# The sample's MLP in another order: product 4 ahead of 6, a down step inside the last pair, a split last block

## The chip, the cores and the metric

The kernel runs on one core of a Trainium2 chip. The metric is the device time of one execution in microseconds (us). A core has five engines that run side by side, each with a queue of its own that it works off strictly in order: TensorE (PE, matrix products into the accumulator memory PSUM, with its weight loads as PEld), VectorE (DVE), ScalarE (ACT), GpSimd (POOL) and SyncE (SP, which here issues the transfers between the core's memory SBUF and DRAM). They wait for each other through semaphores.

## The reference

One encoder layer for two batches, a prompt of 512 tokens and a sample of 1024, with shared weights, all in float32. The model width is 1024, the MLP's inner width D_FF 2816.

```python
h = _rmsnorm(x, norm_attn_g[l])
z = h @ w_in[l]                       # queries, keys, values, two convolution inputs
a_out = _window_attn(q, k, v, bias, band, attn_sink[l])
c = ca * jax.nn.sigmoid(cb)
c = _dwconv(c, conv_dw_w[l], conv_dw_b[l])
c = jax.nn.silu(_layernorm(c, conv_ln_g[l], conv_ln_b[l]))
x = x + jnp.concatenate([a_out, c], axis=-1) @ w_out[l]
h = _rmsnorm(x, norm_ffn_g[l])
u = _dwconv(h @ w_up[l], ffn_dw_w[l], ffn_dw_b[l])        # 3 taps over tokens
x = x + (jax.nn.silu(u[..., :D_FF]) * u[..., D_FF:]) @ w_down[l]
return _rmsnorm(x, norm_final_g)
```

The change lies in the last four lines, for the sample.

## The kernel before

Products are made in float32 accuracy from parts: each operand is split into a rounded part (hi, a cast on ACT) and the rest (lo, a subtraction on DVE or POOL), and a product is hi·hi + hi·lo + lo·hi, three matmuls of 128 x 128 weights by 512 columns. Until 907 us of the profile the kernel works on the input projection, the attention, the convolution, the prompt's MLP and the sample's out-projection. What follows is the sample's MLP.

*Operands.* `scaled` (line numbers below are those of the code shown at the end of this section) scales the normalised token blocks and forms sums and differences of them, since the MLP's big products are made in a scheme of seven half-size products instead of eight: the tokens, the model width, and the pair gate/value (or, in the down stage, the inner width and the output) are each halved, and sums of halves are multiplied. The seven left operands are transposed by PE, four 128 x 128 blocks at a time (`turned`, L961), cast by ACT (L963) and split by DVE (L918); seven right operands come from the weights by `sums_up` (three sums on DVE, one on POOL) and `split_up` (cast on ACT, L1024, rest on POOL, L918).

*Up stage.* The inner width has 22 column blocks of 128 (j, `NJ`). Each has products 1 to 7 of 12 matmuls (`prod`, L1038 to L1040: four slices of the width by three parts). Products 1 and 2 add up in the left half and 4 in the right half of a PSUM tile x; 5 and 3 in the left, 6 and 7 in the right half of a tile wy. There are four such tiles of two banks, named w0 to w3: blocks of even and odd j take turns, so that x of block j+2 needs the place of x of block j, and wy of j+2 that of wy of j. Between products DVE forms sums with L915: u2 (6 with a copy of 1, made by ACT at L1096), u3 (7 with the same copy), and then the halves of gate and value. `gate_part(j)` makes the three taps of the depthwise convolution of x (L1134 on ACT, L1135 and L1136 on DVE) and a tanh (L1143); the second tap of DVE is what frees x. `value_part(j)` does the same for wy (which it frees), multiplies both into t, and after an odd block forms sums of the pair's t and writes ten blocks to a buffer ga in DRAM.

*Down stage.* For seven products i in the order 1, 2, 5, 6, 7, 4, 3 and 11 pairs p of inner blocks (77 steps) `operands` takes the pair's block from ga and a block of w_down, forms differences, and splits both (`split_of`: cast L922, rest L918 on POOL or DVE); a step is 12 matmuls (L1309 to L1311) into two of the wide tiles. `load_next` issues the loads ahead, `make` the splits, four steps ahead. At the end of a product `evacuate` adds into accumulators, and `with_x` the residual.

*Finish.* `finish(blk, ...)` normalises a block of 128 tokens: a square with a sum of each half on ACT (L1359), three small POOL operations (L1360 to L1362), scaling with the final gain (L1366 and L1367 on ACT and POOL for the left half, L1369 on DVE; in the last two blocks both halves by L1369), stores. The last product is worked off by token blocks: first blocks 0 and 1 together with p, then block 2, then block 3.

*What sets the order.* The program is written in the order of the calls, but the Tile framework's scheduler then puts every engine's queue into an order of its own, from its model of durations, and that order is fixed in the program. So the queues as built, not the order of the calls, tell who stands behind whom.

## Time and profile before

| what | us |
|---|---|
| median of 3 runs (lowest to highest) | 1613.76 (1613.69 to 1615.75) |
| the profiled execution | 1611.46 |
| its span on the core | 1609.4 |
| PE busy in it | 1530.8 |
| sample's MLP: product 1 of block 0 starts | at 908.81 |
| product 7 of block 21, in the last pair, starts | at 1360.74 |
| PE's last matmul ends | at 1594.06 |
| mean granted TensorE clock | 0.989 |

Every time in the rows is from the start of the span. A row of the timeline has the start, the duration (both in us), engine, line, operation, out<-in by the program's names, shape and count; in brackets the idle time before it and what ended it. Matmuls overlap in the rows: each lasts about 0.39 us there, but they start about 0.23 us apart. A row of a group has busy us and mean ns behind the bar, then the idle time before such instructions and its releasers. Buffer letters give the size: h is 512 columns in SBUF, q and c 1024, w the wide PSUM tiles.

### The profile page before, as it was taken

How to read it: one execution, taken by the hardware profiler on the slowest of the kernel's cores; microseconds unless marked ns; L12 is line 12 of the kernel's file. 1: busy time of each engine (PE TensorE's matmuls, PEld its weight loads, DVE VectorE, ACT ScalarE, POOL GpSimd, SP SyncE). 2: the span in 40 equal slices, each digit the busy share in tenths (PEclk: the TensorE clock that was granted, in tenths of full speed). 3: DMA queues.
4: the chain of work that ended last, by engine and by line, in shares of the span. 5: the costliest groups of instructions: out<-in, count | busy, mean ns of one | idle time of the engine just before them, and what ended most of it. 6: DMA issues, size and time to landing. Idle time of an engine off the chain costs nothing. (4 is left out here: it accounts for less than half of the span.)

```text
span 1609.4 us, 20236 instructions
## 1 busy us (share of the span) xinstructions
PE 1530.8 (95%) x6907; PEld 1239.3 (77%) x6907; DVE 1194.1 (74%) x1681; ACT 762.5 (47%) x1356; POOL 881.2 (55%) x673
## 2 busy tenths in 40 slices
PE   8899899999999999999899989999999998999996
PEld 6778788877877878888678767777777777887774
DVE  7989857739898987656666768777776767697685
ACT  4634656244566565555443444343333334444353
POOL 6642354147667766556631435665555555455586
PEclk9999999999999999999999999999999999999998
DMA  7572246365233323334572212333333326875512
GB/s 234 151 206 83 79 122 175 96 186 142 86 99 111 106 81 116 105 99 150 171 255 79 79 53 85 98 99 98 98 99 98 99 72 202 307 252 160 173 51 104
DMA packets 209771, 207.62 MB, mean 129 GB/s; under 512 B 11156, under 2 KB 150748, under 8 KB 209541
## 3 DMA queue, kind: packets, MB, share of 16 engines
q1 hardware_dynamic: 209669, 206.35, 40.7%
q8 instruction: 54, 0.88, 0.2%
q14 instruction: 48, 0.39, 0.1%
HBM read 158.84 MB, written 48.51 MB: 129 GB/s over the span
## 5 line engine op out<-in xcount | busy, mean ns | idle before, releaser
L143 POOL TENSOR_TENSOR q<-q,q 128x1024 fp32r<-128x1024 f32 x72 | 174.9, 2435 | 68.2 <-ACT q L142 37.4
L1038 PE MATMUL w<-h,q 128*128 128x512 f32 x516 | 203.9, 395 | 5.0 <-DVE h L915 3.6
L918 POOL TENSOR_TENSOR q<-q,q 128x512 fp32r<-128x512 f32 x107 | 149.9, 1412 | 105.7 <-ACT q L1024 96.7
L1040 PE MATMUL w<-h,q 128*128 128x512 f32 x516 | 200.4, 394 | 0.0
L1039 PE MATMUL w<-h,q 128*128 128x512 f32 x494 | 194.4, 394 | 0.0
L918 DVE TENSOR_TENSOR h<-h,h 128x512 fp32r<-128x512 f32 (+1 forms) x126 | 138.2, 1137 | 48.5 <-ACT h L922 24.3
L249 PE MATMUL u<-h,q 128*128 128x512 f32 x400 | 158.4, 396 | 3.6 <-DVE h L774 2.8
L250 PE MATMUL u<-h,q 128*128 128x512 f32 x400 | 158.4, 396 | 0.6 <-DVE h L211 0.6
L252 PE MATMUL u<-h,q 128*128 128x512 f32 x384 | 152.0, 396 | 1.6 <-POOL q L143 1.6
L918 POOL TENSOR_TENSOR h<-h,h 128x512 fp32r<-128x512 f32 x69 | 104.8, 1534 | 87.1 <-ACT h L922 56.6
L922 ACT CAST h<-h 128x512 fp32r<-128x512 f32 x154 | 88.0, 619 | 113.0 <-DVE h L918 35.4
L292 DVE SCALAR_TENSOR_TENSOR c<-c,cvw,c 128x512 f32<-128x512 f32 x184 | 137.9, 749 | 2.4
L1311 PE MATMUL w<-h,h 128*128 128x512 f32 x308 | 121.6, 395 | 0.0
L1309 PE MATMUL w<-h,h 128*128 128x512 f32 x308 | 120.9, 394 | 0.0
L1310 PE MATMUL w<-h,h 128*128 128x512 f32 x296 | 117.3, 396 | 3.7 <-DVE h L918 3.7
L1038 PEld LDWEIGHTS w<-h,q 128*128 128x128 f32 x516 | 97.5, 189 | 29.0 <-issue 6.9
L1024 ACT CAST q<-q 128x512 fp32r<-128x512 f32 x107 | 65.5, 620 | 111.0 <-PE w L1040 72.0
L1040 PEld LDWEIGHTS w<-h,q 128*128 128x128 f32 x516 | 97.5, 189 | 22.1 <-POOL q L918 0.2
L142 ACT CAST q<-q 128x1024 fp32r<-128x1024 f32 x72 | 75.6, 1049 | 77.2 <-POOL q L143 44.7
L1039 PEld LDWEIGHTS w<-h,q 128*128 128x128 f32 x494 | 93.4, 189 | 20.9
L249 PE MATMUL b<-h,q 128*128 128x512 f32 x256 | 103.6, 405 | 3.5 <-DVE d L322 3.5
L252 PE MATMUL b<-h,q 128*128 128x512 f32 x256 | 101.7, 398 | 0.0
(393 smaller groups left out, 3933.9 us busy)
## 6 DMA issues: line engine op xcount, KB each, us to landing
q<-in_w_up SPq DMA_DIRECT2D x88, 512.0 KB
h<-in_w_down SPq DMA_DIRECT2D x110, 256.0 KB
h<-ga SPq DMA_DIRECT2D x77, 256.0 KB
ga<-q SPq DMA_DIRECT2D x66, 256.0 KB
q<-in_w_in SPq DMA_DIRECT2D x28, 512.0 KB
q<-in_x_sample SPq DMA_DIRECT2D x15, 512.0 KB
...
```

Of the source, the lines that this page charges most:

```text
L143: (nc.vector if dve else nc.gpsimd).tensor_tensor(lo[:], raw[:], hi[:].bitcast(F32), op=ALU.subtract)
L249: nc.tensor.matmul(out, whi[:, kc, :], hi[:], start=(kc == 0), stop=False)
L250: nc.tensor.matmul(out, whi[:, kc, :], lo[:], start=False, stop=False)
L252: nc.tensor.matmul(out, wlo[:, kc, :], hi[:], start=False, stop=(kc == KC - 1))
L292: nc.vector.scalar_tensor_tensor(acc[:], src(t), w(t), acc[:], op0=ALU.mult, op1=ALU.add)
L918: (eng or nc.vector).tensor_tensor(out, a, b, op=ALU.subtract)
L1038: nc.tensor.matmul(out, whi[:, s], hi[:], start=(start and c == 0), stop=False, **go)
L1039: nc.tensor.matmul(out, whi[:, s], lo[:], start=False, stop=False, **go)
L1040: nc.tensor.matmul(out, wlo[:, s], hi[:], start=False, stop=(stop and c == 3), **go)
L1309: nc.tensor.matmul(out, sh[:, c], th[:], start=(p == 0), stop=False)
L1310: nc.tensor.matmul(out, sh[:, c], tl[:], start=False, stop=False)
L1311: nc.tensor.matmul(out, sl[:, c], th[:], start=False, stop=(p == NPAIR - 1))
```

## The change

Five edits, all in the sample's MLP:

- The last of the sums in `scaled` moves, for token blocks b = 0 and 1, into `last_sum`, called after the loop over the out-projection's blocks, and a drain of the side work in that loop is left out.
- The transposes of operands 4, 6, 7 and 5 are written between the matmuls of products 2 and 4 of blocks 0 and 1 (`between`), one group of four after each slice, instead of ahead of them.
- In the loop over j from 2, `fourth(j)` is called before `sixth(j)`.
- The down loop's body becomes `down_step(k)`. Step 0 is called inside the last round of the up loop, after `gate_part(21)` and ahead of `third(21)`; it makes operands one step ahead instead of four.
- For the last two blocks `left_first` squares the left half and multiplies it with the gain ahead of the block's matmuls; `finish` then scales the left half on ACT and the right on DVE, which stores them as before in halves.

```diff
         sub(s2[:], s1[:], e[:, L])
         sub(x[:, L], e[:, L], x[:, L])
-        sub(e[:, L], e[:, R], s2[:])
+        if i >= NB - 2:
+            last_sum(b)
+
+    def last_sum(b):
+        sub(rows[0, b][:, L], rows[0, b][:, R], rows["s2", b][:])
...
-    def prod(out, j, i, start, stop):
+    def prod(out, j, i, start, stop, between=None):
...
             if j == NJ - 1:
                 A.pop((i, c))
+            if between is not None:
+                next(between, None)
...
         for n in range(2):
-            if i == 8 and n == 1:
-                drain(side)
             out_blocks(i, n)
...
     drain(side)
+    for b in range(2):
+        last_sum(b)
     split_up(0, 1, 2)
...
-    turn(4)
-    second(0)
...
-    turn(7)
-    fourth(0)
...
+    t = turn(4)
+    next(t)
+    second(0, t)
+    for _ in t:
+        pass
...
+    t = turn(7)
+    next(t)
+    fourth(0, t)
+    for _ in t:
+        pass
...
-    for j in range(2, NJ):
-        for half in range(2):
-            load_up(j + 3, half)
-        split_up(j + 1, 1, 2)
-        sixth(j)
-        sums_up(j + 1)
-        fourth(j)
-        value_part(j - 1)
-        second(j)
-        seventh(j)
-        split_up(j + 1, 6, 4)
-        fifth(j)
-        if j == NJ - 1:
-            load_next(6)
-        first(j + 1)
-        gate_part(j)
-        third(j)
-        split_up(j + 1, 7, 5, 3)
-    sb.free.extend(raws.free)
-    value_part(NJ - 1)
...
-    fin = None
+    fins = []
+
+    early = {}
+
+    def left_first(tt):
+
+        ss, o = early[tt] = sm(2), sb.tile([D])
+        part = cut(o11, tt)
+        nc.scalar.activation(o[:, L], part, AF.Square, accum_out=ss[:, 0:1])
+        nc.vector.tensor_tensor(part, part, fins[0][:, L], op=ALU.mult)
 
     def finish(blk, parts, tail):
-        ss, rs = sm(2), sm(2)
-        o = sb.tile([D])
-        for n in range(2):
+        ss, o = early.pop(blk) if tail else (sm(2), sb.tile([D]))
+        rs = sm(2)
+        for n in range(1 if tail else 0, 2):
...
             if n == 0 and not tail:
                 nc.scalar.activation(o[:, s], parts[n], AF.Identity, scale=rs[:, 1:2])
...
+            elif n == 0:
+                nc.scalar.activation(o[:, s], parts[n], AF.Identity, scale=rs[:, 1:2])
             else:
...
-    for k, (i, p) in enumerate(steps[:-NPAIR]):
+    pd = []
+
+    def down_step(k):
+        i, p = steps[k]
         load_next(8 if k == 0 else 3 if len(pr) < CAP else 0)
-        make(k + LEAD)
+        make(k + (LEAD if k else 1))
         if p == 0:
-            pd = [wide() for _ in range(2)]
+            pd.extend(wide() for _ in range(2))
...
+    for j in range(2, NJ):
+        for half in range(2):
+            load_up(j + 3, half)
+        split_up(j + 1, 1, 2)
+        fourth(j)
+        sums_up(j + 1)
+        sixth(j)
+        value_part(j - 1)
+        second(j)
+        seventh(j)
+        split_up(j + 1, 6, 4)
+        fifth(j)
+        if j == NJ - 1:
+            load_next(6)
+            gate_part(j)
+            down_step(0)
+        first(j + 1)
+        if j < NJ - 1:
+            gate_part(j)
+        third(j)
+        split_up(j + 1, 7, 5, 3)
+    sb.free.extend(raws.free)
+    value_part(NJ - 1)
+
+    for k in range(1, len(steps) - NPAIR):
+        down_step(k)
...
     for tt in (2, 3):
+        left_first(tt)
         z = wide()
```

The lines of the code shift with it: `prod`'s matmuls become L1042 to L1044, the taps L1140 (ACT), L1141 and L1142 (DVE), the copy of product 1 L1102, the tanh L1149, the down stage's matmuls L1306 to L1308, the transposes L965, the load of down operands L1260, the finish's DVE scaling L1377 and its squares L1357 and L1365; the helpers L915, L918 and L922 keep theirs.

What the scheduler makes of it, at three places. In names with numbers the first part is the buffer, the second counts its tiles: w1_29 is x of block 9, w1_33 x of block 11, w2_32 wy of block 10 and w3_30 wy of block 9; w0_55 is the first down tile, in the place of x of block 20.

First place, around product 1 of block 11 in the up stage. PE before, the end of product 5 of block 9 and the start of product 1 of block 11:

```order
L1038 MATMUL w3_30_10290<-h55_1507_9024,q4_1643_10274 128x512
L1039 MATMUL w3_30_10290<-h39_1508_9025,q4_1643_10274 128x512
L1040 MATMUL w3_30_10290<-h55_1507_9024,q4_1643_10274 128x512
L1038 MATMUL w1_33_10524<-h24_1409_8341,c3_1659_10422 128x512
L1039 MATMUL w1_33_10524<-h41_1410_8342,c3_1659_10422 128x512
L1040 MATMUL w1_33_10524<-h24_1409_8341,c3_1659_10422 128x512
```

PE now, the end of product 7 of block 10 and the start of product 1 of block 11:

```order
L1042 MATMUL w2_32_10445<-h48_1498_8984,q4_1656_10409 128x512
L1043 MATMUL w2_32_10445<-h54_1499_8985,q4_1656_10409 128x512
L1044 MATMUL w2_32_10445<-h48_1498_8984,q4_1656_10409 128x512
L1042 MATMUL w1_33_10524<-h24_1409_8360,c3_1659_10422 128x512
L1043 MATMUL w1_33_10524<-h41_1410_8361,c3_1659_10422 128x512
L1044 MATMUL w1_33_10524<-h24_1409_8360,c3_1659_10422 128x512
```

DVE before, from u3 of block 9 to the second tap of x of block 9, which product 1 of block 11 waits for (q to q at L918 are raw sums of weights):

```order
L915 TENSOR_TENSOR h35_1650_10341<-w3_30_10290,h6_1639_10238 128x512
L915 TENSOR_TENSOR w1_29_10237<-w1_29_10237,h35_1650_10341 128x512
L918 TENSOR_TENSOR q9_24_10133<-q9_24_10133,q8_23_10131 128x512
L915 TENSOR_TENSOR w2_28_10141<-w2_28_10141,h15_1631_10142 128x512
L1135 SCALAR_TENSOR_TENSOR q10_1654_10390<-w1_29_10237,fw_266,q10_1654_10390 128x1023
L918 TENSOR_TENSOR q8_23_10131<-q9_24_10133 128x512
L918 TENSOR_TENSOR q1_21_9993<-q1_21_9993 128x512
L1136 SCALAR_TENSOR_TENSOR q10_1654_10390<-w1_29_10237,fw_266,q10_1654_10390 128x1023
```

DVE now, from u3 of block 9 to the first sum behind the same tap:

```order
L915 TENSOR_TENSOR h60_1650_10341<-w3_30_10307,h15_1639_10238 128x512
L1161 TENSOR_TENSOR q7_1641_10256<-q7_1641_10256,q0_1649_10323 128x1024
L915 TENSOR_TENSOR w1_29_10237<-w1_29_10237,h60_1650_10341 128x512
L1141 SCALAR_TENSOR_TENSOR q10_1654_10390<-w1_29_10237,fw_266,q10_1654_10390 128x1023
L915 TENSOR_TENSOR w3_30_10307<-w3_30_10307,h60_1650_10341 128x512
L1142 SCALAR_TENSOR_TENSOR q10_1654_10390<-w1_29_10237,fw_266,q10_1654_10390 128x1023
L915 TENSOR_TENSOR h15_1662_10446<-w2_32_10445,h17_1653_10376 128x512
```

The raw sums have left the stretch between u3 and the tap, and PE comes to product 1 of block 11 one product 7 later, not straight behind product 5 of block 9. The raw sums stand elsewhere now. DVE now, from two raw sums to the second tap of wy of block 10, which product 6 of block 12 waits for:

```order
L918 TENSOR_TENSOR q1_27_10418<-q11_28_10420 128x512
L918 TENSOR_TENSOR q3_26_10282<-q3_26_10282,q6_25_10280 128x512
L915 TENSOR_TENSOR w2_32_10445<-w2_32_10445,h15_1662_10446 128x512
L918 TENSOR_TENSOR q1_27_10418<-q1_27_10418 128x512
L918 TENSOR_TENSOR q6_25_10280<-q3_26_10282 128x512
L915 TENSOR_TENSOR h17_1678_10595<-w3_34_10594,h6_1669_10525 128x512
L918 TENSOR_TENSOR q6_25_10280<-q6_25_10280 128x512
L1141 SCALAR_TENSOR_TENSOR q10_1679_10610<-w2_32_10445,fw_266,q10_1679_10610 128x1023
L1142 SCALAR_TENSOR_TENSOR q10_1679_10610<-w2_32_10445,fw_266,q10_1679_10610 128x1023
```

DVE before, the stretch to the same tap:

```order
L915 TENSOR_TENSOR w2_32_10428<-w2_32_10428,h11_1661_10429 128x512
L1135 SCALAR_TENSOR_TENSOR q13_1684_10677<-w1_33_10524,fw_266,q13_1684_10677 128x1023
L918 TENSOR_TENSOR q1_27_10418<-q11_28_10420 128x512
L918 TENSOR_TENSOR q6_25_10280<-q6_25_10280 128x512
L1136 SCALAR_TENSOR_TENSOR q13_1684_10677<-w1_33_10524,fw_266,q13_1684_10677 128x1023
L1135 SCALAR_TENSOR_TENSOR q12_1679_10610<-w2_32_10428,fw_266,q12_1679_10610 128x1023
L918 TENSOR_TENSOR q1_27_10418<-q1_27_10418 128x512
L915 TENSOR_TENSOR w3_34_10577<-w3_34_10577,h17_1680_10628 128x512
L1136 SCALAR_TENSOR_TENSOR q12_1679_10610<-w2_32_10428,fw_266,q12_1679_10610 128x1023
```

Three raw sums of blocks 13 and 12 and u2 of block 11 (h17_1678) stand now between the sum of wy of block 10 and its taps, where the taps of x of block 11 and three raw sums stood.

Second place, the last pair (blocks 20 and 21). PE before, the end of product 5 of block 20 and the start of product 7 of block 21 (w3_54 is wy of block 21):

```order
L1038 MATMUL w2_52_11855<-h55_1507_9024,q14_1807_11843 128x512
L1039 MATMUL w2_52_11855<-h39_1508_9025,q14_1807_11843 128x512
L1040 MATMUL w2_52_11855<-h55_1507_9024,q14_1807_11843 128x512
L1038 MATMUL w3_54_11994<-h30_1492_8950,q12_1822_11985 128x512
L1039 MATMUL w3_54_11994<-h38_1493_8951,q12_1822_11985 128x512
L1040 MATMUL w3_54_11994<-h30_1492_8950,q12_1822_11985 128x512
```

PE now, the end of product 2 of block 21 (w1_53) and the start of the first down step:

```order
L1043 MATMUL w1_53_11951<-h23_1467_8702,c2_1810_11852 128x512
L1044 MATMUL w1_53_11951<-h4_1466_8701,c2_1810_11852 128x512
L1306 MATMUL w0_55_12118<-h7_1846_12106,h5_1844_12102 128x512
L1307 MATMUL w0_55_12118<-h34_1847_12107,h5_1844_12102 128x512
L1308 MATMUL w0_55_12118<-h7_1846_12106,h29_1845_12103 128x512
L1306 MATMUL w0_55_12118<-h7_1846_12106,h5_1844_12102 128x512
L1307 MATMUL w0_55_12118<-h34_1847_12107,h5_1844_12102 128x512
```

PE now, the last of these 14 down matmuls and the start of product 7 of block 21:

```order
L1307 MATMUL w0_55_12118<-h42_1851_12115,h13_1848_12110 128x512
L1308 MATMUL w0_55_12118<-h53_1850_12114,h49_1849_12111 128x512
L1306 MATMUL w0_55_12118<-h21_1860_12173,h31_1858_12169 128x512
L1307 MATMUL w0_55_12118<-h14_1861_12174,h31_1858_12169 128x512
L1042 MATMUL w3_54_12006<-h30_1492_8950,q0_1822_11985 128x512
L1043 MATMUL w3_54_12006<-h38_1493_8951,q0_1822_11985 128x512
L1044 MATMUL w3_54_12006<-h30_1492_8950,q0_1822_11985 128x512
```

Product 7 stood straight behind product 5 of block 20; now that product 5, products 4 and 2 of block 21, 3 of block 20, the rest of 6 of block 21 and 14 down matmuls follow one another ahead of it.

Third place, the end of DVE's queue. Before, from the scalings of blocks 6 and 7 on (q10_2150 is the right half's accumulator of blocks 0 and 1, q7_2151 that of 2 and 3, q11_2019 the left half's of 2 and 3):

```order
L1369 SCALAR_TENSOR_TENSOR q14_2317_13998<-q3_2082_13015,s21_2316_13997,q13_2244_13679 128x512
L1369 SCALAR_TENSOR_TENSOR q2_2320_14029<-q3_2082_13015,s23_2319_14028,q13_2244_13679 128x512
L915 TENSOR_TENSOR q10_2150_13296<-w2_67_13865,q10_2150_13296 128x512 x2
L1369 SCALAR_TENSOR_TENSOR q4_2323_14043<-q10_2150_13296,s25_2322_14042,q13_2244_13679 128x512
L1369 SCALAR_TENSOR_TENSOR q9_2326_14057<-q10_2150_13296,s27_2325_14056,q13_2244_13679 128x512
L915 TENSOR_TENSOR q7_2151_13297<-w0_68_14068,q7_2151_13297 128x512
L1369 SCALAR_TENSOR_TENSOR q5_2329_14105<-q11_2019_12746,s29_2328_14104,q13_2244_13679 128x512
L1369 SCALAR_TENSOR_TENSOR q5_2329_14105<-q7_2151_13297,s29_2328_14104,q13_2244_13679 128x512
L915 TENSOR_TENSOR q7_2151_13297<-w3_69_14115,q7_2151_13297 128x512
L1369 SCALAR_TENSOR_TENSOR q8_2332_14152<-q11_2019_12746,s31_2331_14151,q13_2244_13679 128x512
L1369 SCALAR_TENSOR_TENSOR q8_2332_14152<-q7_2151_13297,s31_2331_14151,q13_2244_13679 128x512
```

Now, the same stretch:

```order
L1377 SCALAR_TENSOR_TENSOR q14_2316_13997<-q3_2082_13015,s21_2317_13998,q10_2244_13679 128x512
L1377 SCALAR_TENSOR_TENSOR q2_2319_14028<-q3_2082_13015,s23_2320_14029,q10_2244_13679 128x512
L1358 TENSOR_TENSOR q11_2019_12746<-q11_2019_12746,q10_2244_13679 128x512 x2
L915 TENSOR_TENSOR q13_2150_13296<-w2_67_13865,q13_2150_13296 128x512 x2
L1377 SCALAR_TENSOR_TENSOR q4_2322_14042<-q13_2150_13296,s25_2323_14043,q10_2244_13679 128x512
L1377 SCALAR_TENSOR_TENSOR q9_2325_14056<-q13_2150_13296,s27_2326_14057,q10_2244_13679 128x512
L915 TENSOR_TENSOR q7_2151_13297<-w0_68_14072,q7_2151_13297 128x512
L1377 SCALAR_TENSOR_TENSOR q5_2328_14069<-q7_2151_13297,s29_2329_14107,q10_2244_13679 128x512
L915 TENSOR_TENSOR q7_2151_13297<-w3_69_14120,q7_2151_13297 128x512
L1377 SCALAR_TENSOR_TENSOR q8_2331_14117<-q7_2151_13297,s31_2332_14155,q10_2244_13679 128x512
```

The two products of L1358 are new and stand ahead of the sums of blocks 0 and 1; in the last two blocks one of two scalings is gone from DVE.

38 lines of the change are left out of this document (22 added, 16 removed).

## The prediction

> **What bounds the kernel now.** I read the page's busy rows first, then the waits of PE over the sample's MLP (943 us to the end), then stages, then PE and its releasers in order of time around each wait.
>
> ```profile
> PE 1530.8 (95%) x6907; PEld 1239.3 (77%) x6907; DVE 1194.1 (74%) x1681; ACT 762.5 (47%) x1356; POOL 881.2 (55%) x673
> PE w L1038 <- DVE q L1136: 12.9, 8, 2.4
> PE w L1310 <- DVE h L918: 3.7, 3, 1.9
> PE w L1038 <- DVE h L915: 3.6, 2, 3.3
> 1166.40:1206.70 40.30, 38.85 (x170) 31.46 (x169) 28.45 (x31) 16.12 (x23) 23.96 (x18) 1.00 0.30 98
> ```
>
> PE is the bound, so only its holes can be won. Rows of waits read "us in total, times, longest". The last row is one period of the up stage (two column blocks): the columns are length, then busy PE, PEld, DVE, ACT, POOL, then clock and DMA. 168 matmuls take 38.8 us of 40.3; DVE has 12 us free, so the 1.5 us are not lack of DVE time but its order.
>
> ```profile
> 1126.04 0.40 PE L1040 MATMUL w<-h,q 128*128 128x512 f32 x1
> 1128.02 0.47 PE L1038 MATMUL w<-h,c 128*128 128x512 f32 x1 [1.58 <-DVE q L1136]
> 1128.32 0.39 PE L1039 MATMUL w<-h,c 128*128 128x512 f32 x1
> 1121.91 1.78 DVE L918 TENSOR_TENSOR q<-q,q 128x512 f32<-128x512 f32 x1 [0.68 <-POOL h L918]
> 1124.21 1.27 DVE L1135 SCALAR_TENSOR_TENSOR q<-w,fw,q 128x1023 f32<-128x1023 f32 x1
> 1125.40 1.28 DVE L918 TENSOR_TENSOR q<-q 128x512 f32<-128x512 f32 x2
> 1126.60 1.27 DVE L1136 SCALAR_TENSOR_TENSOR q<-w,fw,q 128x1023 f32<-128x1023 f32 x1
> 1087.59 0.47 PE L1038 MATMUL w<-h,c 128*128 128x512 f32 x1 [2.35 <-DVE q L1136]
> ```
>
> The third kind of row is the place of the eight waits: product 1 of block 11 needs the PSUM tile that the second tap (L1136) of block 9 frees, and that tap ends at 1127.87, behind two raw sums of L918. Matmuls that don't wait start 38.8 / 168 = 0.231 us apart, the pitch used below.
>
> ```profile
> 1356.52 1.82 DVE L918 TENSOR_TENSOR h<-h,h 128x512 fp32r<-128x512 f32 x1
> 1358.26 1.27 DVE L1136 SCALAR_TENSOR_TENSOR q<-w,fw,q 128x1023 f32<-128x1023 f32 x1
> 1359.90 0.69 DVE L915 TENSOR_TENSOR h<-w,h 128x512 f32<-128x512 f32 x1 [0.37 <-DMA ga<-h]
> 1357.00 0.40 PE L1040 MATMUL w<-h,q 128*128 128x512 f32 x1
> 1360.74 0.77 PE L1038 MATMUL w<-h,q 128*128 128x512 f32 x1 [3.35 <-DVE h L915]
> 1366.43 0.52 PE L1039 MATMUL w<-h,q 128*128 128x512 f32 x1
> 1366.78 0.39 PE L1040 MATMUL w<-h,q 128*128 128x512 f32 x1
> 1357.40:1366.70 9.30, 5.96 (x14) 4.73 (x15) 6.50 (x8) 3.33 (x5) 1.34 (x2) 0.63 0.66 222
> ```
>
> This is the last pair: product 7 of block 21 waits 3.35 us for the sum u2 (L915), which waits behind a tap. Then the granted clock is low (0.63 in the stage): 14 pitches from 1360.74 to 1366.78 take 6.04 us instead of 14 x 0.23 = 3.23, so 2.8 more are lost, 6.15 together.
>
> **The change, part by part.**
>
> *Transposes between matmuls, and the late sum.* PE's order there reads alike before and after, so the transposes stay as they are, and so do the pauses between them. The two sums moved behind the loop change the order of some transposes and of the DVE work behind out-projection blocks, with equal counts, and product 1 of block 0 still waits for the last residual add. Both: 0; a moved group could cost or save at most one such pause, 0.4 us (row below).
>
> ```profile
> 943.46 0.50 PE L1038 MATMUL w<-h,h 128*128 128x512 f32 x1 [0.40 <-DVE h L918]
> ```
>
> *Product 4 before 6 in a block.* No instruction is added; the scheduler puts the up stage in another order. Product 1 of block j+2 stands no longer straight behind product 5 of j+1. I walk through one period by duration, t = 0 where product 1 of block 10 begins, product n of a row at its place times 0.231:
>
> ```profile
> L1134 ACT ACTIVATE q<-w,vecs,fw 128x1024 f32<-128x1024 f32 x25 | 30.2, 1208 | 23.3 <-DVE w L915 13.6 <-PE w L1040 9.6
> L1136 DVE SCALAR_TENSOR_TENSOR q<-w,fw,q 128x1023 f32<-128x1023 f32 x24 | 30.6, 1273 | 0.2
> L915 DVE TENSOR_TENSOR w<-w,h 128x512 f32<-128x512 f32 x36 | 24.9, 692 | 0.9
> L918 DVE TENSOR_TENSOR q<-q,q 128x512 f32<-128x512 f32 x18 | 21.6, 1202 | 19.4 <-POOL q L918 14.6 <-POOL h L918 4.8
> L918 DVE TENSOR_TENSOR q<-q 128x512 f32<-128x512 f32 x26 | 17.2, 683 | 0.0
> L918 POOL TENSOR_TENSOR q<-q,q 128x512 fp32r<-128x512 f32 x60 | 83.6, 1405 | 42.4 <-ACT q L1024 38.9 <-PE w L1040 3.5
> ```
>
> Gate half (tile x) of block 10: product 7 ends at 22.1, u3 and its add take 1.4, ACT's L1134 then waits for a slot until the stores of the pair before have landed, near 29, and with 1.21 and two taps of 1.27 the tile is free near 33; product 1 of block 12 wants it at 38.7. Block 11: product 7 ends at 44.3, u3 begins at 45.2, the add ends at 46.6, ACT at 47.8, the taps near 50.5; wanted at 60.9. The old wait is covered by 5 to 10 us. The tight one is now product 6 of block 12, which needs the tile of block 10's products 5 and 3 (wy). Product 3 of 10 ends at 35.7, product 6 of 12 begins 37 matmuls later, at 44.3. Between lie the add (0.69), ACT's L1134 (1.21) with DVE's raw sums beside it (two of 0.68 to 1.20), u2 of block 11 (0.69), one more raw sum that waits for POOL (0.68 to 1.2), and two taps of 1.27: 6 to 7 us where DVE is free at 35.7. It comes about 1.7 late, behind two raw sums for blocks 13 and 12 that wait for a load and for POOL's third sum (1.3 to 1.4 each). I get 44.0 against 44.3: cover of 0.3, stalls of 0 to 1 us in some periods. Of 12.9 us, 0 to 4 remain; I take 2, because most of the means are of work beside POOL already: **-10.9**.
>
> *The start of that stage.* The raw sums of block 5 now stand ahead of u3 of block 2, and wait for POOL's third sum, which waits behind a split that waits for a store of DRAM. Lower bound: -0.5, since an order with fewer sums ahead of taps can also save a short wait. Upper bound: the longest wait that such a queue made for PE in this stage, 2.35 us (the row of 1087.59). I take **+0.5**, nearer the lower end, since POOL is 55% busy over the span and its splits stand earlier in the new order.
>
> *First down step inside the last pair.* Product 5 of block 20 is now followed by 4 and 2 of block 21, product 3 of 20, the rest of 6 and 2 of 21, then 14 down matmuls, and only then 7 of 21. Counted in the same way from product 1 of block 20, 6 of 21 ends at 38.0, u2 (0.69) at about 40.1 behind one split (0.69 to 1.8), and 7 is due at 41.9: the 3.35 us and the slow clock behind them have 14 x 0.231 = 3.2 us of cover. What is late next are the operands of those 14: the first of them needs the load of ga behind six stores on SP's queue, then a cast and a split on POOL.
>
> ```profile
> L922 ACT CAST h<-h 128x512 fp32r<-128x512 f32 x78 | 45.6, 619 | 58.3 <-PE w L1310 14.7 <-POOL h L918 12.0 <-DVE h L918 7.4
> L918 POOL TENSOR_TENSOR h<-h,h 128x512 fp32r<-128x512 f32 x35 | 54.0, 1555 | 51.5 <-ACT h L922 28.4 <-PE w L1310 8.8 <-DVE h L918 4.7
> ACT h L922 <- DMA h<-in_w_down: 5.4, 1, 5.4
> ```
>
> Product 5 of 20 ends at 27.7, its add (0.69) frees the load's slot at 28.4; with three or four transfers ahead of it, 1.2 us each (256 KB at the 222 GB/s of the stage's row above), it lands by 33; it is cast by 36.1 behind other casts, split by 38.1, needed at 39.2. Cover of 1 us; the worst load wait of this stretch is 5.4. So 0 to 4.4 us can come back; I take 0.65: **-5.5**. The four loads of x1 and the eight first loads are only moved on SP's queue. From the ninth step on the order is as before.
>
> *The rest of the down stage.* Same order, same waits. A slow stretch like the one above follows a wait of 1.86:
>
> ```profile
> 1516.66 0.63 PE L1310 MATMUL w<-h,h 128*128 128x512 f32 x1 [1.86 <-DVE h L918]
> 1520.41 0.39 PE L1310 MATMUL w<-h,h 128*128 128x512 f32 x1
> ```
>
> Nine pitches take 3.75 us there instead of 2.07: 1.7 lost. The 2.35 us wait at 1087.59 cost no clock (0.39 a matmul behind it). I take 0; -1.7 if that stretch isn't drawn, +1.7 if another wait draws one.
> [...]
>
> *The tail.* The last two blocks get their left half's product with the final gain on DVE (L1358) ahead of time, so that once the block's norm is known ACT scales left beside DVE right. But the two new products wait for ACT's squares of those blocks, which wait for a free output slot until 1592.64, and on DVE they stand ahead of the sums of blocks 0 and 1:
>
> ```profile
> 1589.67 1.27 DVE L915 TENSOR_TENSOR q<-w,q 128x512 f32<-128x512 f32 x2
> 1592.64 0.63 ACT L1359 ACTIVATE q<-q 128x512 f32<-128x512 f32 x1 [3.95 <-DMA out_sample<-q]
> 1593.96 0.61 ACT L1359 ACTIVATE q<-q 128x512 f32<-128x512 f32 x1
> 1596.97 1.75 DVE L1369 SCALAR_TENSOR_TENSOR q<-q,s,q 128x512 f32<-128x512 f32 x1 [0.44 <-POOL s L1362]
> 1598.64 0.68 DVE L915 TENSOR_TENSOR q<-w,q 128x512 f32<-128x512 f32 x1
> 1602.43 0.68 DVE L915 TENSOR_TENSOR q<-w,q 128x512 f32<-128x512 f32 x1
> 1604.90 1.41 DVE L1369 SCALAR_TENSOR_TENSOR q<-q,s,q 128x512 f32<-128x512 f32 x2 [1.79 <-POOL s L1362]
> ```
>
> These squares run one behind the other from 1592.64 until block 0's begins at 1593.96. The products (0.69 each) then end at about 1594.8, the sums (0.64 each) begin there and not at 1589.67, and block 0's square begins at about 1595.5, not 1593.96: +1.5 for everything behind, since DVE takes the blocks in turn (1596.97, 1598.64, 1602.43). Each of the last two blocks then has one scaling of 0.7 on DVE instead of 1.41: -1.4. The last two stores go out together, one issue of some 0.35 to 0.5 behind the other: +0.5. Sum **+0.6**, from -1.5 (slots free earlier) to +1.5.
>
> Sum: -10.9 + 0.5 - 5.5 + 0.6 = -15.3. The profiled execution took 1611.46 us (span 1609.4 and 2.06 outside), the median of the runs is 1613.76: 1596.2 on the first, 1598.5 on the second. I say **1598**.
>
> **Rivals.**
> 1. *The wait moves to product 6.* If DVE comes to the wy tap 1.5 to 1.9 us later than in my walk, each of eight or nine periods waits 1.2 to 1.6 us: 10 to 13 us come back beside the 2 that I left, and the time is 1606 to 1610. For it: a cover of only 0.3. Against it: DVE has 12 us of 40 free.
> 2. *Slower: raw sums hold up DVE.* Three sums a block now stand ahead of the taps and adds. A sum took 0.68 alone (the group of 26 above) and 1.78 beside POOL (1121.91): 3 x 1.1 = 3.3 us a block, 6.6 a period. Covered are 0.3 of them at product 6; were all 6.6 in that chain, nine periods would lose 57 us. It decides from (15.3 + 3.2) / 9 + 0.3 = 2.4 us a period, 36% of the worst; at half of the worst the loss is 27 us, the time 1625. Against it: the mean of the kind is 1.20, so most of it is in my walk, and some of the sums stand where DVE idles.
> [...]
> 3. *The last pair's operands are late.* Wait and slow clock return at the 14 matmuls: -5.5 becomes 0, the time 1604.
> 4. *No change:* the new order has as many holes as the old, 1611 to 1617.
>
> **How the numbers follow.** My sum 0.62, rival 3 0.11, rival 1 0.10, rival 4 0.06, rival 2 0.11. A measurement tells 0.2% (3.2 us) from no change. Faster: the first three, 0.83; same 0.06; slower 0.11. The sum's own range is 1592 to 1604: its ends are -2 and +2 in the up stage, -0.65 and +3.75 in the last pair, -0.5 and +1.85 at the start, -2.1 and +0.9 in the tail and 1.7 either way for the clock, never all at once; the best, with all of the gains but the clock's, is 1593, with it and a shorter down stage 1590. To reach 8 in 10 I add rivals 3 and most of 1: 1590 to 1609.
>
> **What would show it.** PE waits for L1142 (the tap's new line): from 12.9 us to under 4, none at product 1. No 3.35 us wait by 7(21), clock 1.00 throughout 1320 to 1400. Same waits of 1.3 to 1.9 us in the down stage. Tail behind the last matmul 15.3 us before, about 16 after. The prediction is wrong if there are many waits of product 6 for L1142, or DVE is idle behind POOL's L918 while PE waits.

## The result: no difference that can be told

The changed kernel took 1612.59 us (median of 14 runs, 1609.53 to 1616.81), the kernel before 1613.38 (14 runs, 1609.91 to 1616.71). The ratio is 1.0001 with a 95% interval of 0.9989 to 1.0013. I had forecast 1598. The profiled execution of the change took 1616.81 us, with a span of 1615.0; a second profiled execution of the same kernel (first experiment) had a span of 1609.0. Both are used below, since the first one ran the transposes at a slow clock (0.53 in the mean from 931 to 949 us, 1.00 in the second), which comes and goes between executions of one kernel (last section).

PE's matmuls have another order after the change, but not another number. So the two kernels can be set side by side by counting PE's matmuls from product 1 of block 0 (transposes included, 2852 in all). The table gives the time from the start of one counted matmul to the start of the next one named, read from the traces; the tail runs from the end of the last matmul to the end of the span.

| stretch of PE's matmuls | what it is | before | after | after, again | forecast of the difference | difference (after, again) |
|---|---|---|---|---|---|---|
| 1 to 225 | blocks 0 and 1, transposes | 51.45 | 55.85 | 51.52 | 0 | +4.4, +0.1 |
| 225 to 717 | up stage to product 1 of block 8 | 116.38 | 121.91 | 120.59 | -1.2 (0.5, less the tap wait of 1.7 there) | +5.5, +4.2 |
| 717 to 1725 | up stage to product 1 of block 20 | 243.29 | 239.15 | 239.11 | -7.9 (the six tap waits there, 9.9, less the 2 that I left) | -4.1, -4.2 |
| 1725 to 2001 | last pair, first down steps | 71.35 | 67.19 | 67.43 | -6.8 (-5.5, and the tap wait of 1.3 there) | -4.2, -3.9 |
| 2001 to the last | down stage | 202.39 | 207.41 | 206.17 | 0 | +5.0, +3.8 |
| tail | finish | 15.3 | 16.2 | 16.3 | +0.6 | +0.9, +0.9 |

The second execution adds up to +0.9 us, and it began the sample's MLP 1.3 us earlier, which gives its -0.4 in span. What was won in the long stretch of the up stage and at the last pair was lost at the start of the up stage and in the down stage; that the two sums meet so closely is chance.

The page's busy rows after, and then PE's waits in the sample's MLP, after (us in total, times, longest):

```profile
PE 1540.5 (95%) x6907; PEld 1243.8 (77%) x6907; DVE 1201.1 (74%) x1681; ACT 762.5 (47%) x1358; POOL 882.8 (55%) x673
```

```profile
PE w L1307 <- DVE h L918: 7.6, 4, 3.7
PE w L1042 <- DVE h L915: 4.6, 3, 3.2
PE w L1042 <- DVE q L1142: 2.6, 5, 1.0
PE w L1042 <- ACT q L1140: 1.0, 1, 1.0
PE w L1042 <- ACT q L1028: 0.9, 2, 0.5
```

The wait for the second tap (L1136, now L1142) fell from 12.9 to 2.6 us, as forecast. Beside it the waits for the sums u2 and u3 (L915) are now 4.6 us, where they were 3.6, and those for splits of the down stage 7.6 (L918 behind L1307, the second part of a down matmul), where they were 3.7. Such a wait also costs a little more than its idle time (six of 9.9 us cost 11.0 in the long stretch of before), and behind some the granted clock is low (0.50 from 1426.4 to 1429.9 us, behind the wait of 3.67), so the stretches of the table say more than the sums of waits.

*The start of the up stage.* PE and then DVE, after, around product 5 of block 5:

```profile
1045.16 0.39 PE L1044 MATMUL w<-h,q 128*128 128x512 f32 x1
1048.79 0.80 PE L1042 MATMUL w<-h,q 128*128 128x512 f32 x1 [3.24 <-DVE h L915]
1049.39 0.63 PE L1043 MATMUL w<-h,q 128*128 128x512 f32 x1
```

```profile
1044.28 0.68 DVE L915 TENSOR_TENSOR w<-w,h 128x512 f32<-128x512 f32 x1
1044.88 2.07 DVE L918 TENSOR_TENSOR q<-q 128x512 f32<-128x512 f32 x3
1046.87 1.27 DVE L1141 SCALAR_TENSOR_TENSOR q<-w,fw,q 128x1023 f32<-128x1023 f32 x1
1048.06 0.68 DVE L915 TENSOR_TENSOR h<-w,h 128x512 f32<-128x512 f32 x1
```

In the new order product 5 of block 5 stands directly behind product 7 of block 5, whose place in PSUM it can only fill once u3 has read it. Product 7 ends at 1045.55. At that time DVE is in a row of three raw sums (one of block 7, two of block 6), then comes the first tap of block 4, and only then u3, which ends at 1048.74. The granted clock is at half (0.50) from 1047.6, still inside the wait of 3.24, to 1054.4 (0.63 a matmul in the third PE row).

*The last pair.* PE, after, at the first down matmuls and at product 7 of block 21:

```profile
1364.16 0.50 PE L1308 MATMUL w<-h,h 128*128 128x512 f32 x1 [0.72 <-POOL h L918]
1366.41 0.50 PE L1307 MATMUL w<-h,h 128*128 128x512 f32 x1 [0.83 <-DVE h L918]
1369.23 0.50 PE L1042 MATMUL w<-h,q 128*128 128x512 f32 x1 [0.93 <-DVE h L915]
```

The 3.35 us wait of before and the slow clock behind it are gone (the granted clock is 1.00 from 1323 to 1397 us); three short waits of 2.5 us in all have come in their place.

*The down stage.* PE at the 206th down matmul (step 17), then DVE, then the waits of DVE from 1385 to 1440 and of SP's queue from 1365 to 1425, all after:

```profile
1421.28 0.41 PE L1306 MATMUL w<-h,h 128*128 128x512 f32 x1
1425.35 0.50 PE L1307 MATMUL w<-h,h 128*128 128x512 f32 x1 [3.67 <-DVE h L918]
```

```profile
1416.32 1.89 DVE L918 TENSOR_TENSOR h<-h,h 128x512 f32<-128x512 f32 x3 [2.60 <-DMA h<-in_w_down]
1420.52 0.69 DVE L918 TENSOR_TENSOR h<-h,h 128x512 f32<-128x512 f32 x1 [2.31 <-DMA h<-in_w_down]
1421.84 4.67 DVE L918 TENSOR_TENSOR h<-h,h 128x512 f32<-128x512 f32 x5 [0.62 <-DMA h<-in_w_down]
```

```profile
DVE h L918 <- DMA h<-in_w_down: 7.6, 5, 2.6
```

```profile
SPq L1260 <- POOL h L918: 9.8, 3, 6.5
```

The split that PE waits for was ready at 1419.7, when its block had been cast, but on DVE it stands behind subtractions of w_down blocks for later steps and behind a split of step 20 (the order as built). Those subtractions wait for loads; DVE idles 7.6 us for them, against 1.8 in the same stretch of before:

```profile
DVE h L918 <- DMA h<-in_w_down: 1.8, 3, 0.7
```

SP issues these loads in order, and stands up to 6.5 us for a buffer that a POOL split has to give free (0.9 before).

### The profile page after: what moved, and what is told of

The parts are those of the page before. It is cut to its first block, busy times and chain, and to the rows that moved or that the text cites. A ratio compares the mean times of both kernels' runs of the same rounds, so it can differ in the third digit from the quotient of the medians.

```text
span 1615.0 us, 20218 instructions
## 1 busy us (share of the span) xinstructions
PE 1540.5 (95%) x6907; PEld 1243.8 (77%) x6907; DVE 1201.1 (74%) x1681; ACT 762.5 (47%) x1358; POOL 882.8 (55%) x673
## 5 line engine op out<-in xcount | busy, mean ns | idle before, releaser
L918 POOL TENSOR_TENSOR q<-q,q 128x512 fp32r<-128x512 f32 x107 | 147.3, 1387 | 138.7 <-ACT q L1028 138.6
L1042 PE MATMUL w<-h,q 128*128 128x512 f32 x516 | 203.5, 397 | 10.8 <-DVE h L915 4.6
L1044 PE MATMUL w<-h,q 128*128 128x512 f32 x516 | 201.2, 394 | 0.8 <-POOL q L918 0.8
L918 DVE TENSOR_TENSOR h<-h,h 128x512 fp32r<-128x512 f32 (+1 forms) x126 | 137.8, 1136 | 45.6 <-DMA h<-in_w_down 28.0
L918 POOL TENSOR_TENSOR h<-h,h 128x512 fp32r<-128x512 f32 x69 | 104.9, 1536 | 86.0 <-ACT h L922 61.4
L922 ACT CAST h<-h 128x512 fp32r<-128x512 f32 x154 | 87.3, 618 | 110.6 <-DVE h L918 39.2
L1042 PEld LDWEIGHTS w<-h,q 128*128 128x128 f32 x516 | 97.5, 189 | 38.9 <-issue 8.1
L1307 PE MATMUL w<-h,h 128*128 128x512 f32 x296 | 117.9, 398 | 7.6 <-DVE h L918 7.6
L1308 PE MATMUL w<-h,h 128*128 128x512 f32 x308 | 122.1, 398 | 0.7 <-POOL h L918 0.7
L1306 PE MATMUL w<-h,h 128*128 128x512 f32 x308 | 122.0, 397 | 0.0
L1044 PEld LDWEIGHTS w<-h,q 128*128 128x128 f32 x516 | 97.4, 189 | 23.8 <-POOL q L918 1.7
```

Of the source, the lines that this page charges most:

```text
L918: (eng or nc.vector).tensor_tensor(out, a, b, op=ALU.subtract)
L1042: nc.tensor.matmul(out, whi[:, s], hi[:], start=(start and c == 0), stop=False, **go)
L1044: nc.tensor.matmul(out, wlo[:, s], hi[:], start=False, stop=(stop and c == 3), **go)
L1306: nc.tensor.matmul(out, sh[:, c], th[:], start=(p == 0), stop=False)
L1307: nc.tensor.matmul(out, sh[:, c], tl[:], start=False, stop=False)
L1308: nc.tensor.matmul(out, sl[:, c], th[:], start=False, stop=(p == NPAIR - 1))
```

## Experiments

Each kernel's stretches, in the form of the table above, with the time and the ratio to the kernel before, which was run beside it:

| run | 1-225 | 225-717 | 717-1725 | 1725-2001 | 2001-last | tail | median us | ratio (95%) |
|---|---|---|---|---|---|---|---|---|
| before | 51.45 | 116.38 | 243.29 | 71.35 | 202.39 | 15.3 | | |
| the change again | 51.52 | 120.59 | 239.11 | 67.43 | 206.17 | 16.3 | 1612.69 | 0.9997 (0.9982 to 1.0013) |
| only 4 before 6 | 51.53 | 117.90 | 239.67 | 66.03 | 207.71 | 15.5 | 1610.62 | 0.9979 (0.9961 to 0.9997) |
| not in block 5 | 51.68 | 120.52 | 240.35 | 67.53 | 205.76 | 16.3 | 1612.14 | 0.9994 (0.9979 to 1.0009) |
| inner down step, 6 first | 56.13 | 117.10 | 245.17 | 66.35 | 200.73 | 15.5 | 1609.78 | 0.9976 (0.9960 to 0.9993) |
| that again | 51.56 | 116.48 | 243.85 | 66.34 | 200.83 | 15.4 | 1605.03 | 0.9943 (0.9921 to 0.9966) |
| old tail | 55.04 | 119.01 | 240.17 | 67.85 | 208.29 | 15.4 | 1614.28 | 0.9996 (0.9980 to 1.0011) |
| without 11 subtractions | 54.25 | 120.93 | 238.93 | 67.35 | 205.17 | 16.2 | 1613.30 | 0.9988 (0.9972 to 1.0005) |
| before, without them | 54.21 | 116.42 | 244.57 | 70.15 | 201.44 | 15.3 | 1612.63 | 0.9985 (0.9965 to 1.0005) |
| old tail, them on POOL | 51.48 | 121.82 | 239.20 | 67.28 | 211.58 | 15.4 | 1615.12 | 1.0006 (0.9990 to 1.0022) |
| no loads of x1 | 51.42 | 120.27 | 239.21 | 64.58 | 206.18 | 14.7 | 1612.28 | 0.9975 (0.9955 to 0.9995) |
| 4 first from block 5, old tail | 51.47 | 116.98 | 243.77 | 66.92 | 208.16 | 15.6 | 1614.60 | 1.0000 (0.9979 to 1.0021) |
| sums of block 7 on 384 columns | 51.82 | 120.64 | 238.47 | 66.94 | 208.52 | 16.2 | 1614.35 | 0.9988 (0.9965 to 1.0010) |

The stretches are of one profiled execution each. Down the column of the down stage the kernels part in two groups: the nine rows with product 4 first take 205.2 to 211.6 us (the first execution of the change 207.41), the four with product 6 first 200.7 to 202.4.

### The change once more

> The changed kernel once more, for a second trace. Theory 1 (the waits belong to the order): the 3.2 us wait of product 5 of block 5 behind product 7 of block 5 and the 3.7 us wait near the 11th to 18th down step come back at the same matmuls, each with a slow clock of 3.4 to 6.8 us behind it, and the time is 1610 to 1616. Theory 2 (they are chance): one or both are missing, and then this execution is 5 us or more under 1615 of span. The slow clock of 17 us over the transposes (931 to 949) is expected to be chance by both: missing here more likely than not.

No edit. It shows which stretches of the first profiled execution belong to the kernel: the 55.85 us of the first stretch became 51.52, the wait at block 5 stayed (2.97 us), the down stage stayed long. Its waits came at the 206th down matmul again (1.90 us) and at the 398th (2.19), this time without a slow clock behind them (1.00 from 1390 to 1470 us).

### Product 4 before 6, alone

```diff
-        sixth(j)
-        sums_up(j + 1)
         fourth(j)
+        sums_up(j + 1)
+        sixth(j)
```

> The kernel before with nothing changed but product 4 ahead of product 6. As built, its up stage has the same order on PE as the changed kernel, and 7 down matmuls already stand ahead of product 7 of block 21 (14 in the changed kernel). Theory 1: the swap carries the whole gain at the pairs and nearly all in the last pair: waits for the tap 2 to 4 us instead of 12.9, the 3.2 us wait at block 5 there, last-pair wait under 2 us, down-stage wait there or not; time within 2 us of the changed kernel. Rival: the last pair's gain belongs to the inner down step; then 3 us and a slow clock are back at product 7 of block 21.

On top of the kernel before. Three lines alone took away the 3.35 us wait of the last pair (71.35 to 66.03), as much as the inner down step does: as built, products of block 21 and seven down matmuls stand ahead of product 7 of block 21 there, without any edit of the down loop. The periods of the up stage gained 3.6 us. The down stage lost 5.3, with 4.7 us of waits of PE between 1385 and 1480, where the kernel before has 1.3:

```profile
PE w L1309 <- ACT h L922: 1.9, 1, 1.9
PE w L1310 <- DVE h L918: 1.5, 1, 1.5
PE w L1311 <- DVE h L918: 1.3, 1, 1.3
```

So the down stage's loss comes with the order of 4 and 6 and not with the down step that was moved. Together with the start (+1.5, with a wait of 1.99 us at product 5 of block 5) it leaves about 2 us of 9.

### The change without block 5

```diff
-        fourth(j)
+        (fourth if j != 5 else sixth)(j)
         sums_up(j + 1)
-        sixth(j)
+        (sixth if j != 5 else fourth)(j)
```

> The changed kernel, except that block 5 alone keeps product 6 ahead of product 4; as built, product 1 of block 6 then stands between products 7 and 5 of block 5. Theory 1 (product 5 waits for u3, which stands on DVE behind three raw sums and a tap): the 3.2 us wait shrinks to 0.5 or less and the slow clock of 6.8 us behind it goes, together 5 to 6 us: 1607 in the median where the changed kernel has 1612.6. Rival (DVE is late for the whole start of the stage): the wait turns up at another product of blocks 4 to 7, 2 to 3 us of it, and the time is as before.

The 3.24 us wait went, and two others came, so that the stretch is as long as before that edit (120.52 against 120.59). PE between 1035 and 1100:

```profile
1037.60 0.47 PE L1042 MATMUL w<-h,q 128*128 128x512 f32 x1 [1.66 <-DVE h L915]
1045.32 0.50 PE L1042 MATMUL w<-h,q 128*128 128x512 f32 x1 [1.97 <-DVE h L915]
```

The first is product 7 of block 5, which waits for u2; the second is product 5 of block 5, which still waits for u3 although product 1 of block 6 now stands between it and product 7. So the place directly behind product 7 is not the cause in itself. DVE is late in that whole stretch, as the rival said, and the product that needs its next sum shows it.

### The inner down step without product 4 first

```diff
-        fourth(j)
-        sums_up(j + 1)
         sixth(j)
+        sums_up(j + 1)
+        fourth(j)
...
-    for tt in (2, 3):
-        left_first(tt)
...
```

The tail is the old one too; transposes, late sum and `down_step(0)` in the last round stay.

> The changed kernel with product 6 ahead of 4 again and the old finish of the last two blocks: what is left are the transposes, the late sum and the down step inside the last pair. As built, product 7 of block 21 stands straight behind product 5 of block 20 again. Theory 1 (the swap makes the gain): tap waits of 12.9 us and the 3.3 us wait of product 7 of block 21 are back; time 1612 to 1616. Rival (the inner step makes the last pair's gain): the 3.3 us wait and its slow clock are gone, 6 us less than the kernel before: 1607.

> The same kernel as in the run of the last pair alone (0.9976 [0.9960, 0.9993] there). Theory A: what it has over the full change is the order on DVE in the down steps 9 to 22, where the split of step 17 stands directly behind that of step 16 and ahead of step 20's; then matmul 100 to 412 of the down product take 72 us again without a wait over 0.5, and the time is 1608 to 1611, ratio 0.996 to 0.999. Rival: that run was luck with the slow clock and with the loads, and 0.9976 came from it; then the ratio is 0.999 to 1.001 and a wait of 1.5 to 3.5 us is seen between steps 16 and 35.

PE's waits over the sample's MLP in the second of the two runs, and its waits for loads on DVE from 1385 to 1440:

```profile
PE w L1042 <- DVE q L1142: 12.8, 8, 2.3
PE w L1307 <- DVE h L918: 2.5, 2, 2.0
PE w L1042 <- DVE w L915: 0.6, 1, 0.6
```

```profile
DVE h L918 <- DMA h<-in_w_down: 0.4, 1, 0.4
```

The tap waits are back in full (12.8), and still this has the lowest times of all kernels tried. Of the first expectation the rival came true (the wait of 3.3 us and its slow clock are gone, with a granted clock of 1.00 from 1326 to 1399 us), if with 1609.78 us and not 1607; of the second theory A, with a time even below its range. In the second run it is 5.0 us less in the last pair and 1.6 less in the down stage than the kernel before, with 0.6 more in the up stage. Product 7 of block 21 stands directly behind 5 of block 20 there, as before, and doesn't wait; its sum u2 (L915) now stands ahead of the two taps on DVE and not behind them, as DVE's rows of the same run show:

```profile
1354.63 0.69 DVE L915 TENSOR_TENSOR h<-w,h 128x512 f32<-128x512 f32 x1 [2.25 <-DMA ga<-h]
1355.23 1.27 DVE L1141 SCALAR_TENSOR_TENSOR q<-w,fw,q 128x1023 f32<-128x1023 f32 x1
```

So here the wait went with the other place on DVE, and not with the cover by down matmuls on which I had counted. Windows of 312 down matmuls, from behind the 100th, show the down stage by itself, in the kernel before, the change, and this one (length, busy PE, PEld, DVE, ACT, POOL, clock, DMA share, GB/s):

```profile
1397.74:1471.23 73.49, 72.15 (x313) 58.50 (x312) 60.70 (x62) 31.43 (x52) 38.20 (x24) 1.00 0.70 235
```

```profile
1397.43:1474.77 77.34, 73.67 (x313) 59.63 (x312) 66.70 (x68) 32.22 (x55) 42.62 (x26) 0.98 0.71 239
```

```profile
1391.86:1463.85 71.99, 71.99 (x314) 58.60 (x312) 59.29 (x63) 32.73 (x55) 37.30 (x24) 1.00 0.71 247
```

312 matmuls at the free pitch are 72 us, which the last row has. In the changed kernel DVE has 68 instructions and is busy 6 to 7 us more in this stretch than in the other two, and POOL 4 to 5 us more: PE comes to it with more of the up stage's work on DVE and POOL still undone. In the two runs the ratio was 0.9976 and 0.9943, with intervals that barely meet; both are below 1. What of the difference between them is chance is taken up in the last section.

### The change with the old tail

```diff
-        ss, o = early.pop(blk) if tail else (sm(2), sb.tile([D]))
-        rs = sm(2)
-        for n in range(1 if tail else 0, 2):
+        ss, rs = sm(2), sm(2)
+        o = sb.tile([D])
+        for n in range(2):
...
-        left_first(tt)
```

> The changed kernel with the old finish of the last two blocks, nothing else undone. Theory 1 (two products on DVE ahead of blocks 0 and 1, and a second store behind each): from PE's last matmul to the end of the span about 15.4 us as in the kernel before, 0.8 less than the changed kernel's 16.2, and the time 1611.8 where the changed kernel has 1612.6. Rival (the end is set by the stores of the earlier blocks): 16.2 as in the changed kernel.

The tail is 15.4 instead of 16.2 to 16.3 us; the rest is that of the change within its scatter. A gain of 0.8 us is too small for the times to show.

### Subtractions of the fifth down product left out, or moved

```diff
-            sub(b[:], pr[B12, p][:], b[:])
```

In the fifth of the down stage's products (`i` is 7) the 11 subtractions of w_down blocks are left out, in the change and in the kernel before; the operand is then the plain block. In the third kernel they stay, but run on POOL (`sub(..., nc.gpsimd)`), with the old tail.

> The changed kernel without the differences of w_down blocks for product 7 of the down stage (the 11 subtractions on DVE are left out, the block is split as loaded). Theory 1 (the operands of steps 17 to 34 are made by DVE at a pace that PE can't outrun, so time gained ahead of them is given back in waits): the waits near down matmuls 206, 398 and 410 shrink from about 4.5 us in all to 1.5 or less, and matmul 412 comes 3 us or more earlier after matmul 100 than in the changed kernel (77.4): 74 or less; time 1608 to 1610. Rival (these waits are for loads from DRAM): they stay, within 0.5 us, and the time is as the changed kernel's.

> The kernel before without the same 11 subtractions. By theory 1 the kernel before has less to win, since its PE comes later: only the 1.3 us wait at matmul 410 goes, 1 to 1.5 us in the time. If the subtractions cost the kernel before as much as the changed one (3 us or more), the time given back isn't due to PE's coming earlier.

> The changed kernel with the old finish and with product 7's 11 differences on POOL instead of DVE. Theory 1: DVE is relieved as in the run that leaves them out, POOL has the room (52 of 101 us busy in this stretch before), the waits at 206, 398 and 410 shrink to 2 us or less, time 1608 to 1610, the first kernel of this series clear of the one before. Rival: POOL's slower work (1.3 to 1.6 us each) makes the splits on POOL late instead, new waits of 2 us or more for POOL's L918, time as before.

With 11 instructions less on DVE, and some of them ahead of the late splits, the stretch 2001 to the last is 205.17 us instead of 206.2 to 207.4 in the change, and 201.44 instead of 202.39 in the kernel before: about as much in both, so these subtractions are not what the two differ by. From the 100th to the 412th down matmul alone it is 74.7 us instead of 77.3 to 77.5 in the change, and 71.9 instead of 73.5 in the kernel before: there a quarter of the 4 us between the two goes with the subtractions, and three quarters stay. PE's wait around step 17 became shorter, and did not go:

```profile
PE w L1306 <- DVE h L918: 1.7, 1, 1.7
```

On POOL they made things worse (211.58): POOL's splits are then late as well, as the rival said (a wait of 2.1 us for one). DVE's queue is part of the cause, but not these instructions alone.

### No loads of x1

```diff
     def load_x1(t, n):
-        xd[t, n] = pair2()
-        ...
+        pass
...
-        x = xd.pop((t, n))
+        x = acc[name]
```

> The full change without the 16 loads of x1 (4 MB, about 11 us of the DMA engines at 375 GB/s, issued between 1330 and 1446); the residual adds of x1 stay on their engines but take the accumulator itself a second time, so the sum is another one. Theory A (order on DVE and ACT: the split of step 17 stands behind subtractions for later steps): the wait at matmul 206 of the down product stays at 1.5 to 3.7 us, matmul 100 to 412 take 76 to 78 us, time 1611 to 1614. Theory B (DMA engines are full from 1380 to 1420, the late loads hold everything up): with 11 us less to transfer no wait over 0.7 at 206 and none at steps 33 and 34, matmul 100 to 412 in 72 to 73.5, time 1607 to 1610, ratio 0.996 to 0.998.

Where x1 was added, the accumulator itself is now added. PE between 1394 and 1418, then waits of DVE from 1385 to 1440, then windows of 20 us:

```profile
1395.67 0.50 PE L1306 MATMUL w<-h,h 128*128 128x512 f32 x1 [1.05 <-DVE q L1142]
1408.79 0.50 PE L1308 MATMUL w<-h,h 128*128 128x512 f32 x1 [2.10 <-DVE h L918]
```

```profile
DVE h L918 <- DMA h<-in_w_down: 4.8, 6, 1.8
```

```profile
1380.00:1400.00 20.00, 18.95 (x83) 15.05 (x82) 14.76 (x12) 9.82 (x17) 11.38 (x8) 1.00 0.77 265
1400.00:1420.00 20.00, 16.32 (x67) 12.49 (x66) 13.42 (x18) 6.74 (x11) 4.93 (x4) 0.97 0.83 293
```

The DMA engines were full in the change (0.96 and 1.03 in the same windows) and are not here, and still DVE idles 4.8 us for loads and PE waits 4.7 us, only at the 119th, 166th and 195th down matmul instead of the 206th. The down stage is as long as in the change (206.18). The DMA engines were just as full in the same windows of the kernel before (0.95 and 0.98) and of the inner step with product 6 first (1.03 and 0.98), which don't wait there. Full DMA engines are not the cause, as theory A had it; why these loads come late is not tested. The place that theory A gave was wrong, since the order on DVE shifts with every such edit. The last pair got 2.8 us faster, so there the x1 loads, or the buffers that they take, seem to cost something.

### Product 4 first only from block 5

```diff
-        fourth(j)
+        (fourth if j >= 5 else sixth)(j)
         sums_up(j + 1)
-        sixth(j)
+        (sixth if j >= 5 else fourth)(j)
```

> Product 4 first only from block 5 on, the tail as before, all else of the change kept. Theory A (the start of the stage cost 3 to 5 us because raw sums of blocks 6 and 7 stand ahead of u3 of block 5, and what is won before the down product's 100th matmul is given back by its 412th): no wait over 1.7 before block 8, waits and small delays of the up stage 8 to 11 us in place of 12.5 to 13.7, but matmul 100 to 412 still 76 to 79 us, and the time 1610 to 1613, ratio 0.998 to 1.000. Rival (the start of the stage is all that stood in the way): matmul 100 to 412 within 74 and the time 1606 to 1609.

The start is nearly that of before (116.98 against 116.38), as theory A had it; but a wait of 2.48 us for u3 then stands at product 5 of block 7, in the next stretch, which therefore gains nothing (243.77): the wait was moved behind the stage's start, not removed, and that part of theory A is wrong. That the down stage stays long (208.16) is much as it said; the time, 1614.6, is above its range.

### Smaller raw sums of block 7

```diff
             g0, g1, v0, v1 = (block_up(j, half, k) for half in range(2) for k in range(2))
+            if j == 7:
+                v0, v1, g0, g1 = (y[:, :384] for y in (v0, v1, g0, g1))
```

> The full change with the raw sums of block 7 on 384 of 512 columns (the other columns of its operands are not summed); matmul order as in the full change. Theory A: the wait of product 5 of block 5 (3.24 in the profiled execution of the change, 2.97 to 3.17 in four others) is the queue of raw sums ahead of u3, three of them of block 7 and about 3 us long, so it becomes 2.2 to 2.7. Rival: u3 is late for another reason (the load of block 6, POOL's third sum), and the wait stays at 2.9 to 3.3. Time by both: 1611 to 1614.

PE's wait, and DVE ahead of it:

```profile
1048.41 0.79 PE L1044 MATMUL w<-h,q 128*128 128x512 f32 x1 [3.15 <-DVE h L915]
```

```profile
1044.49 0.69 DVE L915 TENSOR_TENSOR w<-w,h 128x512 f32<-128x512 f32 x1
1045.09 1.47 DVE L918 TENSOR_TENSOR q<-q 128x512 f32<-128x512 f32 x2
1046.48 1.27 DVE L1143 SCALAR_TENSOR_TENSOR q<-w,fw,q 128x1023 f32<-128x1023 f32 x1
1047.67 0.68 DVE L915 TENSOR_TENSOR h<-w,h 128x512 f32<-128x512 f32 x1
```

The wait hardly moved (3.15), against theory A. What still stands ahead of u3 when product 7 ends (1045.26) are the two full sums of block 6 and the first tap of block 4: 1.3 + 1.2 + 0.7 us to the end of u3, which is the wait. Block 7's sums were not the piece that mattered.

## Why the prediction was wrong

**The likeliest case did not come; rival 4, no change, did.** I gave it too little since I walked one period and took it for the stage. Four terms of the sum failed: the start of the stage and the down stage were put at about nothing and cost most, the other two were too large. Set against the second execution the start is off by 5.4 us, the down stage by 3.8, the long stretch by 3.7 and the last pair by 2.9.

*The start of that stage, "+0.5"*: this step failed, with +5.9 us in place of it: the stretch is 4.2 longer, though the tap wait of 1.7 in it went (5.5 longer in the first execution; half clock for 3.4 us in the second and 6.8 in the first is in these figures). I had bounded it by 2.35 us, the longest wait that DVE's queue made for PE before; the new wait is 3.24, and two smaller ones come with it. What I saw was raw sums of block 5 ahead of u3 of block 2; the place where it cost was block 5's own product 5, directly behind its product 7, which the steady order never has. That this place alone doesn't make the cost, the run without block 5 shows (waits of 1.66 and 1.97 instead); what makes DVE late in the first blocks is not settled.

*Product 4 before 6, "-10.9"*: right in its mechanism (the tap waits fell to 2.6 us), wrong in size. In the stretch 717 to 1725 I had 7.9 of it, and 4.2 came. 1008 matmuls at 0.2305 us, the mean distance in before of those that don't wait, are 232.3; before lost 11.0 to that, and the change still loses 6.8, where my 7.9 would have left 3. The rest are some ten waits of 0.1 to 1.6 us at products 6 and 7 of a block, which I put at 0 to 1 "in some periods". Rival 1 named product 6 rightly and put its price too high.

*First down step inside the last pair, "-5.5"*: the stretch got 3.9 to 4.2 shorter, where it should have got 6.8 shorter with the tap wait of 1.3 that went in it too. The 3.35 us wait and the slow clock went (0.63 from 1357.4 to 1366.7 us before, 1.00 from 1323 to 1397 now); 1.55 us of waits for the operands of the first down matmuls came back, where I had 0.65 and bounds of 0 to 4.4, and 0.93 at product 7. I had not seen that the order of 4 and 6 cures the same wait by itself (-5.3 alone, -5.0 for the inner step alone, -4 for both).

*The rest of the down stage, "same order, same waits", 0*: this step failed as well, with +3.8 to +5.0. The order is not the same. As built, and counting steps from 0, PE works off steps 11 to 14 ahead of 8 to 10 in the kernel before, and in the change 8 and part of 9 ahead of 11; only from step 16 on, the 193rd down matmul, do the two agree. On DVE they agree from about step 23: there the split of step 17 stands behind both of step 20's, where it stood behind one. I took the stage's order from its later steps.

These places are not the whole cause. With the swap alone PE's steps follow each other as in the kernel before, and the split of step 17 stands behind one of step 20's; still the stage loses 5.3 us. What all kernels with product 4 first share is the end of the up stage: as built, the last product of block 21 stands behind 61 to 66 down matmuls, against 33 in the kernel before and 24 with the inner step and product 6 first. DVE's last subtraction of the up stage follows from it. Its row before, after, and with the inner step again:

```profile
1395.91 0.68 DVE L918 TENSOR_TENSOR q<-q,q 128x512 f32<-128x512 f32 x1
```

```profile
1403.92 0.69 DVE L918 TENSOR_TENSOR q<-q,q 128x512 f32<-128x512 f32 x1
```

```profile
1383.17 0.68 DVE L918 TENSOR_TENSOR q<-q,q 128x512 f32<-128x512 f32 x1
```

The 100th down matmul starts at 1397.5, 1397.2 and 1391.6 in these three. So DVE ends the up stage 1.6 us ahead of it before, 6.7 behind it after, and 8.5 ahead with the inner step. Over all fourteen profiles it is 5 to 10 us behind with product 4 first, and 1.6 to 8.5 ahead with 6 first. It is not that PE comes too early: from product 1 of block 2 to the 100th down matmul it takes 437.3 us before, 433.3 to 434.4 in the change, and 432.9 with the inner step alone, which doesn't pay.

The kernels with product 4 first all pay in this stage (205.2 to 211.6 us), those with 6 first don't. That it comes from the order is shown; that the late end of the up stage on DVE, or SP's late loads, are the link is read from traces and was not tested by itself.

*The tail, "+0.6"*: right, +0.9. The place was as told: the squares wait for output slots, the products with the gain stand behind them, and the sums of blocks 0 and 1 behind these. ACT and DVE, after:

```profile
1597.48 0.63 ACT L1357 ACTIVATE q<-q 128x512 f32<-128x512 f32 x1 [3.96 <-DMA out_sample<-q]
1598.24 1.38 DVE L1358 TENSOR_TENSOR q<-q,q 128x512 f32<-128x512 f32 x2 [3.65 <-ACT q L1357]
1599.53 1.28 DVE L915 TENSOR_TENSOR q<-w,q 128x512 f32<-128x512 f32 x2
```

*Transposes and the late sum, 0*: right; with an equal clock (1.00 from 931 to 949 us in both) the stretch is 51.52 against 51.45.

*Rivals 2 and 3*: raw sums did hold up DVE, at the start and not in every period, so rival 2's loss did not come; the operands of the last pair were late by 1.55 us, not by 5.5.

*Sums of the prediction that don't come out*: rival 1's 10 to 13 us on top of my sum would give 1608 to 1611, not 1606 to 1610, and the start's bounds allow -1.0 below my +0.5, not -0.5. Neither touches the forecast.
